# Short-convolution output product by Strassen's algorithm, with block sums by accumulating DMAs

## The chip, the core and the metric

The program runs on one core of one Trainium2 chip. A core has engines that work side by side, each on its own list of instructions in a fixed order: TensorE (PE, matrix products into the accumulators called PSUM), VectorE (DVE, elementwise work on two tensors), ScalarE (ACT, elementwise functions of one tensor), GpSimd (POOL), and SyncE (SP, which here only issues transfers). Transfers between memory and the on-chip store SBUF, or within SBUF, are done by 16 DMA engines; SP's queue and POOL's queue both issue to them. An instruction that needs another engine's result waits for a semaphore, and everything behind it on its own engine waits too.

The metric is device microseconds of one execution, as the median of several runs. Lower is better.

## What is computed

The reference is a two-layer decoder trunk in float32 on 512 tokens of 1024 features. Layer 0 has an attention block and a gated MLP, layer 1 a gated short convolution and a gated MLP; each is added to the residual stream `h`. The change touches only the last line of this function, the product with `w_out` (1024 x 1024):

```python
def short_conv_mixer(h, norm_g, w_in, conv_w, w_out):
    xn = rms_norm(h, norm_g)
    proj = xn @ w_in
    gate_b = proj[..., :CONV_WIDTH]
    gate_c = proj[..., CONV_WIDTH:2 * CONV_WIDTH]
    u = proj[..., 2 * CONV_WIDTH:]
    y = gate_b * causal_dwconv(gate_c * u, conv_w)
    return y @ w_out
```

and `h = h + short_conv_mixer(...)` around it.

## The kernel before

Activations stay in SBUF with features on the 128 partitions and the 512 tokens along the free axis, so 1024 features are eight tiles of [128, 512]. A float32 product is made of three single-pass products of halves: a number is its rounding to a shorter format (`hi`) plus the exact remainder (`lo`), and `mm3` (lines 235 to 240) adds `w_hi x_hi`, `w_hi x_lo` and `w_lo x_hi` into one PSUM accumulator. So each pair of a 128 x 128 weight block and a 512-column activation tile costs three matrix products on PE, each with its own load of stationary weights.

Weights come in float32 in chunks of 512 KB. All chunks are listed in order of use (`want`, lines 207 and 345 to 380). `weights` (line 229) hands out the next one, and keeps two more in preparation: `load` (line 210) issues the transfer on SP's queue (L220), ACT rounds the chunk to `whi` (L223), DVE takes the remainder `wlo` (L226). Each of raw chunk, `whi` and `wlo` has three buffers, used in turn; a buffer that is still read makes the next writer wait.

The short convolution is lines 812 to 843. Its first loop runs over the eight feature tiles; each tile needs three chunks of the input projection (parts u, c and b), every one of them 24 products into one PSUM bank. Then `mix` (lines 816 to 828) multiplies by the row of RMS scales, does the gating and the three-tap convolution on DVE and ACT, and splits the result into `y_hi` and `y_lo` (L320 on ACT, L321 on DVE). The second loop, lines 837 to 842, is the output product: for each of eight output tiles one chunk of `w_out` and 8 x 3 products of 512 columns into one bank (`psa` and `psb` in turn). `residual_out` (line 764) adds the bank to `h` (L765) and feeds the next block's norm (`Norm.feed`, lines 256 to 265): ACT scales and rounds the tile to `hs_hi` (L258), DVE takes the remainder `hs_lo` (L259), ACT squares it (L264) and DVE adds the squares up (L265). `norm.finish` then has the squares summed over features by small products (L292) and the scales spread over the partitions (L278) while the next stage, the up-projection of the second MLP (`up`, line 774), is already running on `hs_hi` and `hs_lo`.

There are eight PSUM banks: two of tag `a`, four of `b`, two of `c`.

What sets the order of the work: `spend` counts an assumed time of the emitted products, and `after` places small work behind a given amount of it. The list of each engine is then fixed when the program is built. A planner goes through the written instructions, and with its own assumed costs puts on each engine the earliest written one that it holds to be ready. So the order on ACT and DVE isn't always the written one: in the profile the scaling of part u of the last feature tile (L819) runs at 798.45 us, ahead of the remainder of a chunk (L226, 799.36 us) whose loading is written before it. On the chip the planned order is kept, whatever the real durations are.

The functions that the diff touches, and what calls them:

Of the kernel before, what the change touches and what calls it, by code (L numbers as in the profile page):

```python
# [49 lines left out]
def trunk(  # L50
# [48 lines left out]
    # a row a column of `gains`: the norms after the first and the conv taps  # L99
# [105 lines left out]
    wanted, ready, at = [], [], [0]  # L205

    def want(dram, k0, nk, c0, n, *more):
        wanted.append((dram, k0, nk, (c0, n) + more))
# [26 lines left out]
    def mm3(acc, w, rhs, first, last):  # L235
        """acc += w.T @ rhs of two pairs of halves."""
# [10 lines left out]
    class Norm:  # L247
        """Gathers the squares of a block's input and gives its RMS scale by token:
        `col` [token, block] on partitions and `row` along the free axis on all of them."""
# [33 lines left out]
        def scaled(self, fn):  # L283
            """Runs what needs `row` when it is there."""
# [14 lines left out]
    def rsqrt(dst, v, n, name):  # L299
        """dst = v ** -0.5 by Newton's method."""  # L300
# [22 lines left out]
    def causal_conv(dst, src, tap):  # L323
        """dst[t] = tap(2) src[t] + tap(1) src[t-1] + tap(0) src[t-2]."""
# [52 lines left out]
    for o in range(ND):  # L377
        want(conv_w_out[0], 0, 8, o * P, P)
# [14 lines left out]
    # ================= attention =================  # L393
# [4 lines left out]
    def choose():  # L398
        """Columns of 0 and 1 that pick the rows of `dl` and `dr`."""
# [25 lines left out]
    def log_gate():  # L425
        """The gates' log-sigmoid, its running sums on the partitions of `dl`."""
# [70 lines left out]
    def queries_keys(p):  # L497
        """Halves of the normed, gained keys and queries of heads 2p and 2p+1. A
        stick-breaking query keeps its scale apart, by token."""
# [63 lines left out]
    def logits(p, b):  # L563
        """Scores and decay of heads 2p and 2p+1 for 128 queries, and what follows up to the weights."""
# [44 lines left out]
    def turn(p, b, ws):  # L609
        """The weights, keys on partitions, in halves."""  # L610
# [19 lines left out]
    def weigh(p, half):  # L630
        """Weights by both halves of the values at once: a head's product has the one
        half on 64 partitions and the other on the rest, which are then added."""
# [98 lines left out]
    # decay: F_q - F_k of a forgetting head as a product of four rows by four. Head  # L731
# [173 lines left out]
```

## Time and profile before

| | |
|---|---|
| time, median of 3 runs (lowest, highest) | 1234.54 us (1233.63, 1237.62) |
| span of the profiled execution, first to last instruction | 1231.8 us |
| time of the profiled execution outside the span | not recorded apart; the median is 2.7 us above the span |
| busy PE / DVE / ACT / POOL | 1214.5 / 762.9 / 500.7 / 21.5 us |
| granted PE clock, mean | 0.997 |
| DMA moved | 108.13 MB, 88 GB/s on average |

Three ways of reading are needed. The profile's page lists groups of instructions by source line, engine and tiles, as out<-in, with the busy time and the mean duration. The timeline lists single instructions by start time in microseconds from the start of the span. A view of windows gives, for a stretch of time, how long each engine was busy. Durations of PE rows are pipelined: two products that follow each other overlap in the rows, and the distance of their starts tells what one costs. On DVE and ACT, too, an instruction can start a little before its predecessor's row ends.

### The profile page before, as it was taken

To read this page: it belongs to the slowest core of one execution; us is meant where nothing else is said; L and a number is where in the kernel's file an instruction comes from. 1 tells how busy PE (TensorE), PEld (TensorE's weight loads), DVE (VectorE), ACT (ScalarE), POOL (GpSimd) and SP (SyncE) were. 2 spreads that over 40 slices of the span, in tenths; PEclk is the share of its full clock that TensorE was granted. 3 is DMA by queue.
4 is the path that set the end of the run, shared out by engine and by line. 5 is a ranking of instruction groups with operands and counts; after the bars stand their busy time and mean duration, and the time that the engine had idled before them with its cause. 6 is when DMAs were issued, how large, how long until landed. Compare 5 with 4: busy or idle time off the path is not lost.

```text
span 1231.8 us, 14998 instructions
## 1 busy us (share of the span) xinstructions
PE 1214.5 (99%) x5861; PEld 987.9 (80%) x5861; DVE 762.9 (62%) x1256; ACT 500.7 (41%) x779; POOL 21.5 (2%) x104
## 2 busy tenths in 40 slices
PE   8999999999999999999999999999999999999998
PEld 7887878767888888888888888888888888888886
DVE  5786878887776777673333555555767776762222
ACT  6455665655443434342222222233444434342120
POOL 3000000000000000000000000000000000000000
PEclk9999999999999999999999999999999999999999
DMA  6312121212333332323333333332333333322330
GB/s 177 104 36 69 36 69 36 69 52 69 95 93 100 89 102 86 103 79 95 94 94 101 91 97 99 89 101 87 91 98 92 96 95 93 98 91 86 118 105 35
DMA packets 183463, 108.13 MB, mean 88 GB/s; under 512 B 4604, under 2 KB 176684, under 8 KB 183392
## 3 DMA queue, kind: packets, MB, share of 16 engines
q1 hardware_dynamic: 183136, 107.01, 29.5%
q8 instruction: 46, 0.75, 0.3%
q0 software_dynamic: 256, 0.16, 0.1%
q14 instruction: 25, 0.20, 0.0%
HBM read 105.06 MB, written 2.10 MB: 87 GB/s over the span
## 4 chain that ended last, share of the span: by engine, by line
PE 94%; DVE 4%; ACT 1%; DMA 1%; issue 0%; SPq 0%; DVEq 0%; ACTq 0%
PE psa L237 13%; PE psa L239 13%; PE psa L238 13%; PE psb L237 11%; PE psb L239 11%; PE psb L238 11%; PE psa L480 3%; PE psa L482 3%; PE psa L481 3%; PE psb L481 2%; PE psb L480 2%; PE psb L482 2%; PE psb L576 1%; DVE rest L603 1%; PE psc L623 1%; PE psa L642 1%
## 5 line engine op out<-in xcount | busy, mean ns | idle before, releaser
L223 ACT ACTIVATE whi<-raw 128x1024 fp32r<-128x1024 f32 (+1 forms) x198 | 208.3, 1053 | 365.9 <-PE psb L238 127.0
L226 DVE TENSOR_TENSOR wlo<-raw,whi 128x1024 fp32r<-128x1024 f32 (+1 forms) x198 | 240.1, 1213 | 162.3 <-ACT whi L223 161.4
L237 PE MATMUL psa<-hs_hi,whi 128*128 128x512 f32 x544 | 220.4, 405 | 0.5 <-DVE o L653 0.5
L239 PE MATMUL psa<-hs_hi,wlo 128*128 128x512 f32 x544 | 215.5, 396 | 0.0
L238 PE MATMUL psa<-hs_lo,whi 128*128 128x512 f32 x544 | 215.0, 395 | 0.0
L237 PE MATMUL psb<-hs_hi,whi 128*128 128x512 f32 x480 | 189.9, 396 | 0.0
L239 PE MATMUL psb<-hs_hi,wlo 128*128 128x512 f32 x480 | 189.8, 395 | 0.0
L238 PE MATMUL psb<-hs_lo,whi 128*128 128x512 f32 x480 | 188.8, 393 | 0.0
L328 DVE SCALAR_TENSOR_TENSOR u<-y,taps,u 128x510 f32<-128x510 f32 (+1 forms) x176 | 131.0, 747 | 3.0
L239 PEld LDWEIGHTS psa<-hs_hi,wlo 128*128 128x128 f32 x544 | 102.2, 188 | 24.0
L237 PEld LDWEIGHTS psa<-hs_hi,whi 128*128 128x128 f32 x544 | 102.7, 189 | 21.8 <-PE psb L582 0.6
L238 PEld LDWEIGHTS psa<-hs_lo,whi 128*128 128x128 f32 x544 | 102.6, 189 | 21.4
L238 PEld LDWEIGHTS psb<-hs_lo,whi 128*128 128x128 f32 x480 | 90.1, 188 | 21.4
L239 PEld LDWEIGHTS psb<-hs_hi,wlo 128*128 128x128 f32 x480 | 90.1, 188 | 21.4
L237 PEld LDWEIGHTS psb<-hs_hi,whi 128*128 128x128 f32 x480 | 90.3, 188 | 20.3
L779 DVE TENSOR_TENSOR y<-psb,nrow_n 128x512 f32<-128x512 f32 x44 | 30.4, 691 | 83.9 <-PE psb L239 83.9
L320 ACT ACTIVATE a<-u 128x512 fp32r<-128x512 f32 x44 | 27.8, 633 | 118.7 <-DVE u L784 118.7
L783 ACT ACTIVATE u<-u 128x512 f32<-128x512 f32 x44 | 27.8, 632 | 91.4 <-DVE u L328 91.4
L325 ACT ACTIVATE u<-y,taps 128x512 f32<-128x512 f32 x88 | 62.9, 717 | 0.0
L321 DVE TENSOR_TENSOR a<-u,a 128x512 fp32r<-128x512 f32 x44 | 30.4, 692 | 29.4 <-ACT a L320 29.4
L480 PE MATMUL psa<-whi,hs_hi 128*128 128x256 f32 (+1 forms) x128 | 38.6, 303 | 0.0
L482 PE MATMUL psa<-whi,hs_lo 128*128 128x256 f32 (+1 forms) x128 | 36.2, 283 | 0.0
(226 smaller groups left out, 1851.0 us busy)
## 6 DMA issues: line engine op xcount, KB each, us to landing
raw<-in_ffn_w_up SPq DMA_DIRECT2D x88, 512.0 KB, 3.8
raw<-in_ffn_w_down SPq DMA_DIRECT2D x30, 512.0 KB, 3.7
raw<-in_attn_w_in SPq DMA_DIRECT2D x24, 512.0 KB, 3.9
raw<-in_conv_w_in SPq DMA_DIRECT2D x24, 512.0 KB, 3.8
raw<-in_ffn_w_down SPq DMA_DIRECT2D x16, 448.0 KB, 3.7
raw<-in_attn_w_out SPq DMA_DIRECT2D x8, 512.0 KB, 3.4
raw<-in_conv_w_out SPq DMA_DIRECT2D x8, 512.0 KB, 3.9
x_tok<-in_x SPq DMA_DIRECT2D x4, 512.0 KB, 7.9
```

The lines of the kernel that those rows point to most:

```text
L223: made = act.activation(hi[:, 0:nk * n], raw[:, 0:nk * n], AF.Copy)
L226: dve.tensor_tensor(lo[:, 0:nk * n], raw[:, 0:nk * n], f32(hi[:, 0:nk * n]), op=ALU.subtract)
L237: pe.matmul(acc, w[0], rhs[0], start=first, stop=False)
L238: pe.matmul(acc, w[0], rhs[1], start=False, stop=False)
L239: pe.matmul(acc, w[1], rhs[0], start=False, stop=last)
L321: dve.tensor_tensor(lo, src, f32(hi), op=ALU.subtract)
L325: act.activation(dst, src, AF.Copy, scale=tap(2))
L328: dve.scalar_tensor_tensor(dst[:, d:], src[:, 0:S - d], tap(j), dst[:, d:], op0=ALU.mult, op1=ALU.add)
L480: pe.matmul(acc, lhs[0], w[0], start=first, stop=False)
L481: pe.matmul(acc, lhs[0], w[1], start=False, stop=False)
L482: pe.matmul(acc, lhs[1], w[0], start=False, stop=last)
L779: dve.tensor_tensor(y, acc, norm.row, op=ALU.mult)
```

## The change

The output product is no longer 8 x 8 x 3 products of 512 columns. It is done in four units, each for two output tiles. In a unit the weights are seen as 2 x 2 blocks (even and odd feature tiles by left and right output tile; a block is four 128 x 128 tiles deep), and the activations as 2 x 2 blocks too (even and odd feature tiles by left and right 256 tokens). Strassen's algorithm, in the form that reuses partial sums, makes the four result blocks from seven block products instead of eight. A block product is 4 x 3 products of 256 columns.

- Activation side (`token_forms`): for each of the four pairs of feature tiles, four sums of blocks are made on DVE (`minus`), and seven forms of 256 columns are split into halves: rounding on ACT, remainder on DVE. They replace `y_hi` and `y_lo` and serve all four units.
- Weight side (`Unit`): four transfers of 256 KB on SP's queue bring the four blocks, into five buffers used in turn. The four sums s1 to s4 are made by two means: ACT copies a block negated (`negative`), and a transfer on POOL's queue adds one SBUF tile onto another (`add`, an accumulating DMA). Seven blocks of a unit are then split into halves, 512 columns at a time, with six buffers each for `hi` and `lo`.
- Result side (`unit_products`): seven block products go into halves of four PSUM banks. ACT copies one, and DVE adds the parts onto the two tiles of `h`. The norm is fed with both tiles after the unit.
- Order: unit 0 is loaded after the fourth feature tile of the first loop, and its sums and halves are written behind the sixth and seventh. The next unit's loads are written at the start of a unit; its sums and halves stand at three points (`steps`) between the block products and after the last. In unit 0 the first three quarters of four block products are emitted ahead of everything that needs the last pair of feature tiles (`early` = 3).
- The eight chunks of `w_out` leave the list of chunks, so `weights` prepares the chunks of the second MLP two ahead from the last input products on.

The rest of the diff takes out comments.

```diff
@@ want
-    for o in range(ND):
-        want(conv_w_out[0], 0, 8, o * P, P)
@@ new
+    HALF = S // 2
+    LEFT, RIGHT = slice(0, HALF), slice(HALF, S)
+    TOKEN_SIDE = {"b11": 0, "b21": 1, "b22": 2, "t1": 3, "t2": 4, "t3": 5, "t4": 6}
+    class Unit:
+        def __init__(self, pool_, dram, k0, n, c0, name):
+            self.pool, self.n, self.name, self.raw, self.halves = pool_, n, name, {}, {}
+            rows = dram[k0 * P:(k0 + 2 * n) * P, c0:c0 + 2 * P].rearrange("(k two p) c -> two p k c", two=2, p=P)
+            for key, half, c in (("s1", 0, 1), ("a11", 0, 0), ("a22", 1, 1), ("a12", 1, 0)):
+                t = pool_.tile([P, 4, P], F32, tag="raw", name=f"raw{key}_{name}", bufs=5)
+                self.raw[key] = t[:, 0:n, :]
+                nc.sync.dma_start(self.raw[key], rows[half, :, :, c * P:(c + 1) * P])
+        def negative(self, key, other, tag, bufs):
+            t = work.tile([P, S], F32, tag=tag, name=f"raw{key}_{self.name}", bufs=bufs)
+            self.raw[key] = t.rearrange("p (k c) -> p k c", c=P)[:, 0:self.n, :]
+            act.activation(self.raw[key], self.raw[other], AF.Copy, scale=-1.0)
+        def add(self, key, other):
+            nc.gpsimd.dma_start(self.raw[key], self.raw[other], accum_op=ALU.add)
+        def sums1(self):
+            self.negative("s3", "s1", "u1", 3)
+            self.negative("s2", "a11", "u1", 3)
+            self.add("s1", "a22")
+            self.add("s3", "a11")
+        def sums2(self):
+            self.add("s2", "s1")
+        def sums3(self):
+            self.negative("s4", "s2", "u0", 2)
+            self.add("s4", "a12")
+        def split(self, *keys):
+            for key in keys:
+                hi, lo = self.halves[key] = [
+                    self.pool.tile([P, 4, P], F32R, tag=n, name=f"{n}{key}_{self.name}", bufs=6)[:, 0:self.n, :]
+                    for n in ("hi", "lo")]
+                act.activation(hi, self.raw[key], AF.Copy)
+                dve.tensor_tensor(lo, self.raw[key], f32(hi), op=ALU.subtract)
+    def token_forms(pool_, hi, lo, even, odd):
+        t = pool_.tile([P, 4, HALF], F32, tag="sums", name="sums", bufs=1)
...
+        first, second = halves_(0, 1, even[:, LEFT]), halves_(1, 3, odd)
+        minus(0, even[:, RIGHT], even[:, LEFT])
+        minus(2, odd[:, RIGHT], even[:, RIGHT])
+        first()
+        second()
+        minus(1, odd[:, RIGHT], t[:, 0, :])
+        minus(3, odd[:, LEFT], t[:, 1, :])
+        halves_(3, 5, flat(t, 0, 2))()
+        halves_(5, 7, flat(t, 2, 4))()
+    def product(acc, unit, a, b, forms, ks=None):
+        w, i = unit.halves[a], TOKEN_SIDE[b]
+        for k in ks or range(unit.n):
+            hi, lo = (x[:, i, :] for x in forms[k])
+            pe.matmul(acc, w[0][:, k, :], hi, start=k == 0, stop=False)
+            pe.matmul(acc, w[0][:, k, :], lo, start=False, stop=False)
+            pe.matmul(acc, w[1][:, k, :], hi, start=False, stop=k == unit.n - 1)
+            spend(0.36)
+    def unit_products(unit, forms, o, name, steps, early=0):
+        x, z = bank("a"), bank("a")
+        w, y = bank("b"), bank("b")
...
+        four = ((z[:, LEFT], "a11", "b11"), (x[:, LEFT], "a12", "b21"), (w[:, LEFT], "s3", "t3"), (y[:, RIGHT], "s1", "t1"))
+        for acc, a, b in four if early else ():
+            product(acc, unit, a, b, forms, range(early))
...
+        rest(0)
+        act.activation(p1u2[:, LEFT], z[:, LEFT], AF.Copy)
+        rest(1)
+        steps[0]()
+        rest(2)
+        product(z[:, RIGHT], unit, "s2", "t2", forms)
+        plus(p1u2[:, RIGHT], z[:, RIGHT], p1u2[:, LEFT])
+        onto(o, slice(0, S), p1u2)
+        plus(u3, w[:, LEFT], p1u2[:, RIGHT])
+        steps[1]()
+        rest(3)
+        both = h[:, o + 1, :].rearrange("p (i c) -> p i c", i=2)
+        plus(both, u3[:, None, :].to_broadcast([P, 2, HALF]), both)
+        product(x[:, RIGHT], unit, "s4", "b22", forms)
+        onto(o, slice(0, S), x)
+        steps[2]()
+        product(y[:, LEFT], unit, "a22", "t4", forms)
+        onto(o, RIGHT, y[:, RIGHT])
+        onto(o + 1, slice(0, S), y)
@@ mix
-            split(y_hi[:, o, :], y_lo[:, o, :], t)
+            mixed_[o] = t
+            if o % 2:
+                token_forms(mp, *forms[o // 2], mixed_[o - 1], t)
@@ first loop
+            if o == 3:
+                unit(0)
+            if o == 5:
+                units[0].sums1()
+            if o == 6:
+                units[0].sums2()
+                units[0].split("a11", "a12", "s3")
+        units[0].split("s1", "s2")
+        units[0].sums3()
         norm = Norm("n3", 8)
-        for o in range(ND):
-            w = weights()
-            acc = bank("ab"[o % 2])
-            for k in range(ND):
-                mm3(acc, (w[0][:, k, :], w[1][:, k, :]), (y_hi[:, k, :], y_lo[:, k, :]), k == 0, k == ND - 1)
-            residual_out(o, acc, norm)
+        for u in range(4):
+            nxt = u + 1 if u < 3 else None
+            if nxt:
+                unit(nxt)
+            def step0():
+                units[u].split("s4")
+                if nxt:
+                    units[nxt].sums1()
+                units[u].split("a22")
+            def step1():
+                if nxt:
+                    units[nxt].sums2()
+                    units[nxt].split("a11", "s3")
+            def step2():
+                if nxt:
+                    units[nxt].sums3()
+            unit_products(units[u], forms, 2 * u, f"co{u}", (step0, step1, step2), 0 if u else 3)
+            if nxt:
+                units[nxt].split("a12", "s2", "s1")
+            for o in (2 * u, 2 * u + 1):
+                norm.feed(o, h[:, o, :])
         norm.finish()
```

`onto(tile, cols, src)` adds `src` to a tile of `h`, `plus` is a DVE addition, `halves_` a rounding on ACT that returns the function which takes the remainder on DVE, and `rest(i)` emits what `early` left of the i-th of the `four` block products.

More of the change, by code (lines that the diff above doesn't have):

```diff
@@ new lines, in product, with plus, onto, rest @@
+    def product(acc, unit, a, b, forms, ks=None):
[9 more added lines that the diff above has]
+        w, y = bank("b"), bank("b")
+        p1u2 = work.tile([P, S], F32, tag="sq", name=f"p1u2_{name}")
+        u3 = work.tile([P, S], F32, tag="nrow", name=f"u3_{name}", bufs=1)[:, LEFT]
+        def plus(dst, src, other):
+            dve.tensor_tensor(dst, src, other, op=ALU.add)
+        def onto(tile_, cols, src):
+            plus(h[:, tile_, cols], src, h[:, tile_, cols])
+        four = ((z[:, LEFT], "a11", "b11"), (x[:, LEFT], "a12", "b21"), (w[:, LEFT], "s3", "t3"), (y[:, RIGHT], "s1", "t1"))
+        for acc, a, b in four if early else ():
+            product(acc, unit, a, b, forms, range(early))
+        def rest(i):
+            acc, a, b = four[i]
+            product(acc, unit, a, b, forms, range(early, unit.n))
+        rest(0)
[17 more added lines that the diff above has]
+        onto(o + 1, slice(0, S), y)
@@ L813, in trunk, with unit @@
     with tc.tile_pool(name="mix", bufs=1) as mp:
-        y_hi = mp.tile([P, ND, S], F32R, tag="y_hi", name="y_hi")
-        y_lo = mp.tile([P, ND, S], F32R, tag="y_lo", name="y_lo")
+        forms = [[mp.tile([P, 7, HALF], F32R, tag=f"y{n}{k}", name=f"y{n}{k}") for n in ("hi", "lo")] for k in range(4)]
+        units, mixed_ = {}, {}
+        def unit(u):
+            units[u] = Unit(mp, conv_w_out[0], 0, 4, 2 * u * P, f"co{u}")
         def mix(o, accs, norm):
```

7 lines of the change are left out of this document (added).

## Prediction

> **What bounds the kernel now.** I read the page first, then the stretch that the change replaces (the output product of the short convolution), then single instructions of each engine in it.
>
> ```profile
> span 1231.8 us, 14998 instructions
> PE 1214.5 (99%) x5861; PEld 987.9 (80%) x5861; DVE 762.9 (62%) x1256; ACT 500.7 (41%) x779; POOL 21.5 (2%) x104
> DVE 5786878887776777673333555555767776762222
> PE 94%; DVE 4%; ACT 1%; DMA 1%; issue 0%; SPq 0%; DVEq 0%; ACTq 0%
> ```
>
> TensorE (PE) sets the time: 94% of the chain that ended last. The third row, VectorE (DVE) by fortieths of the span, never shows more than 8 tenths; that will matter. The span is 1231.8 us, the median of the runs 1234.54: I take 2.7 us lying around the span as unchanged, and add the change of the span to the median.
>
> The first product of `y_hi` and the first product of the next stage (`hs_hi`) enclose the stage:
>
> ```profile
> 809.41 0.40 PE L237 MATMUL psa<-y_hi,whi 128*128 128x512 f32 x1
> ...
> 853.91 0.39 PE L239 MATMUL psb<-y_hi,wlo 128*128 128x512 f32 x1
> 854.14 0.39 PE L237 MATMUL psa<-hs_hi,whi 128*128 128x512 f32 x1
> ```
> ```profile
> core 0: us, PE busy (x) PEld busy (x) DVE busy (x) ACT busy (x) POOL busy (x), PEclk, DMA share, GB/s
> 809.41:854.14 44.73, 44.73 (x193) 36.09 (x192) 24.79 (x31) 17.11 (x24) 0.00 (x0) 1.00 0.33 96
> ```
>
> 192 products of 512 columns (8 tiles x 8 blocks x 3) take 44.73 us, 0.233 us from start to start, at the full granted clock, without a gap. DVE is busy 24.79 of it, ScalarE (ACT) 17.11. The "0.39" of a row is its pipelined duration; only the distance between starts is a price.
>
> **The change: TensorE.** Four units of seven block products replace this; a block product is 4 blocks x 3 products of 256 columns, so 4 x 7 x 12 = 336. The 256-column price is shown in the attention stage, 17 distances between these two:
>
> ```profile
> 83.28 0.28 PE L480 MATMUL psa<-whi,hs_hi 128*128 128x256 f32 x1
> ...
> 85.29 0.28 PE L482 MATMUL psa<-whi,hs_lo 128*128 128x256 f32 x1
> ```
>
> (85.29 - 83.28) / 17 = 0.118 us. 336 x 0.118 = 39.7 us: **5.0 us saved**, all there is to win. A unit lasts 84 x 0.118 = 9.93 us, a block product 1.42.
>
> **VectorE.** Back to back, DVE operations start closer than their durations; the prices are the distances here:
>
> ```profile
> 866.70 0.69 DVE L779 TENSOR_TENSOR y<-psa,nrow_n 128x512 f32<-128x512 f32 x1 [2.19 <-ACT nrow_n L279]
> 867.31 0.68 DVE L779 TENSOR_TENSOR y<-psb,nrow_n 128x512 f32<-128x512 f32 x1
> 867.91 1.22 DVE L226 TENSOR_TENSOR wlo<-raw,whi 128x1024 fp32r<-128x1024 f32 x1
> 869.04 2.73 DVE L328 SCALAR_TENSOR_TENSOR u<-y,taps,u 128x511 f32<-128x511 f32 x4
> ...
> 828.43 0.74 DVE L259 SCALAR_TENSOR_TENSOR hs_lo<-h,gains,hs_hi 128x512 fp32r<-128x512 f32 x1
> 829.10 0.68 DVE L265 TENSOR_TENSOR nacc_n<-nacc_n,sq_n 128x512 f32<-128x512 f32 x1
> ```
> ```profile
> L653 DVE TENSOR_TENSOR o<-psa,o x32: 392/422/428, 76.3 to 283.9; 64x256 f32<-64x256 f32 x32
> ```
>
> 512 columns cost 0.61, 1024 cost 1.13, the scaled remainder L259 0.67; 256 columns last 0.42, and with the 0.08 that the others gain back to back, 0.34. Before, each pair of output tiles had two residual adds, two 1024-column remainders and the norm's feed: 2 x 0.61 + 2 x 1.13 + 2 x (0.67 + 0.61) = 6.0 us in 11.2. In a unit after it are seven remainders (7 x 0.61 = 4.27), four adds of 512 (2.44), three of 256 (1.02) and the feed (2.56): **10.3 us against TensorE's 9.93**. In the last unit there is no next one to prepare, five remainders go: 7.2. So in three units DVE is the longer engine by 0.36, 1.1 us together. Lower bound 0 (remainders may run ahead in slack; unit 0 has five made before the stage), upper bound under the rivals.
>
> [...]
>
> **ScalarE.**
>
> ```profile
> 873.10 0.62 ACT L320 ACTIVATE a<-u 128x512 fp32r<-128x512 f32 x1
> 873.63 0.71 ACT L325 ACTIVATE u<-y,taps 128x512 f32<-128x512 f32 x1
> ...
> 827.16 0.71 ACT L258 ACTIVATE hs_hi<-h,gains 128x512 fp32r<-128x512 f32 x1
> 827.78 0.61 ACT L264 ACTIVATE sq_n<-h 128x512 f32<-128x512 f32 x1
> ```
>
> Seven roundings and three negations at 0.53, a copy of 256 (some 0.3), the feed 2 x (0.62 + 0.53): 7.9 of 9.93 us. Not the bound, but in order: a rounding that waits for a DMA (s4) holds the negations of the next unit and the rounding of a22. Behind it on DVE a remainder without its rounding holds the adds that free the banks of `x` and `z`, which the next unit's second and first products want; on POOL the sum into s1, waiting for its loads, holds those into s3 and s2.
>
> **The last pair's token sums.** They follow the last gate, which stays:
>
> ```profile
> 809.61 0.69 DVE L826 TENSOR_TENSOR cb<-psb,nrow_n 128x512 f32<-128x512 f32 x1 [1.57 <-PE psb L239]
> 810.34 0.69 DVE L827 TENSOR_TENSOR ct<-ct,cb 128x512 f32<-128x512 f32 x1
> ```
>
> The odd tile is there at 811.03. In written order DVE then makes two differences, two remainders and two more differences (4 x 0.34 + 0.34 + 0.61, with some 0.2 of dependence: 813.5); ACT rounds the last (0.63, 814.2) and DVE takes the remainder (0.69): 815.0 with the hand-overs. TensorE has 36 early products (4.26 us, to 813.7) and 6 more before the first that needs it (814.4). Stall 0.6 in written order, 0 if the even tile's part runs earlier: **0.5**. The forms of pairs 0 to 2 and unit 0's loads, sums and halves lie under the input projection, costed at nothing; there DVE is busy 80.75 of 158.00 us, ACT 42.67:
>
> ```profile
> 651.00:809.00 158.00, 158.00 (x688) 127.94 (x687) 80.75 (x109) 42.67 (x48) 0.00 (x0) 1.00 0.33 96
> ```
>
> Without that cover each pair's forms would cost up to the 4 us just counted (811.03 to 815.0).
>
> **The weight sums.** Nothing in this trace accumulates by DMA. The nearest rows:
>
> ```profile
> raw<-in_conv_w_out SPq DMA_DIRECT2D x8, 512.0 KB, 3.9
> out<-r SPq DMA_DIRECT2D x8, 256.0 KB, 2.0
> spare<-in_ffn_conv POOLq DMA_DIRECT2D x4, 33.0 KB, 3.2
> f_bias<-in_attn_f_bias POOLq DMA_DIRECT2D x1, 4.0 KB, 6.3
> spare<-in_ffn_norm POOLq DMA_DIRECT2D x1, 8.0 KB, 1.8
> L107 POOL DMA_DIRECT2D f_bias<-in_attn_f_bias x1 | 0.7, 726 | 0.0
> ```
>
> Call A the time from issue to landing of one sum of 256 KB. It cannot reasonably beat the plain 256 KB store, 2.0; the longest landing of POOL's queue is 6.3. I take **3.3**, by the row it is nearest to in queue and length (3.2). POOL's 0.7 per issue is inside; four a unit are 2.9 of 9.93 us. Per unit three sums hang on each other: s1 += a22, s2 += s1, s4 += a12, and the next but one unit's A11 can only be loaded into s1's buffer when the second has landed. From a unit's start: loads 4.5 (3.9 for 512 KB and a third block behind), two sums 2A, a negation 0.6, a sum A, rounding and remainder 1.4. s4 is needed in the sixth product of the next unit, at 9.93 + 5 x 1.42 = 17.0. Later units add a round each: two blocks loaded (3.5), 2A, 0.5 of hand-overs. The last unit's s4 is then there at 4.5 + 2A + 2 x (4.0 + 2A) + 2.0 + A = 14.5 + 7A, and needed at 17.0 + 2 x 9.93 = 36.9. **Loss 7A - 22.4 above A = 3.2**: 0.7 us at 3.3, 0 at 2.0, 21.7 at 6.3. These late sums and the DVE surplus fall in the same units, and while TensorE waits DVE catches up; I count the larger, 1.1.
>
> [...]
>
> **What moves at no cost.** Eight chunks of the output weights leave the list, so the first two chunks of the next MLP load and split under the last input products, and its third at the MLP's start: 3.8 us of landing, 1.06 and 1.22 of splitting, for a product 11.2 us later (two of 5.6). SP's queue in the stage then holds only unit loads, so their waits delay nobody else. At the end two tiles instead of one are fed at once:
>
> ```profile
> raw<-in_ffn_w_up SPq DMA_DIRECT2D x88, 512.0 KB, 3.8
> ...
> 854.34 0.69 DVE L765 TENSOR_TENSOR h<-psb,h 128x512 f32<-128x512 f32 x1 [2.23 <-PE psb L239]
> ```
>
> Adds of 0.34 and 0.61, rounding 0.62, remainder and feed 0.67 + 0.61 + 0.67 put the last half some 3.7 us behind the last product; the next stage wants it after 21 products, 4.9 us. Late by 1.2 more, it would cost.
>
> **Sum.** -5.0 + 0.5 + 1.1 = -3.4: 1228.4 us of span, **1231.1 us**.
>
> **Rivals.**
> - *Clean*: the remainders run ahead, A is under 3.2. Only 0 to 0.5 is lost: 1229.5 to 1230.0. For it: DVE has 7.2 us in the last unit. Against: 0.36 a unit too much by the rows.
> - *Slow sums* (the other side): the round of load, s1, s2 paces the units. From A = 3.84 on the loss eats the 4.5 us left; at A = 4.5 it is 9.1 and the time 1239.1, at 5.0 12.6 and 1242.6. For it: 6.3 on POOL's queue, and an in-order ACT behind a late s4. Against: 1.8 and 3.2 on the same queue with 2.0 for the bytes.
> - *VectorE-bound with gaps*: its operations depend on ACT, TensorE and DMA in turn; no fortieth of the span shows it above 8 tenths. At 90% a unit takes 10.3 / 0.9 = 11.4: three times 1.5 lost and 0.5, 1234.5, no change.
> - *Nothing gained by 256 columns* (the change would not do what it says): it would need 0.133 us a product; the rows show 0.118. Under 2%, not counted.
>
> **How the numbers follow.** Forecast 0.40, clean 0.22, slow sums 0.25, gaps 0.13. About 0.3% (3.7 us) is what a measurement can tell from no change. The forecast lies just inside it: two fifths of its chance (0.16) and clean make faster 0.38. Same: the rest of the forecast 0.24, gaps 0.13, and 0.03 of slow sums that end near zero: 0.40. Slower 0.22. The range runs from clean less the 0.9 us by which the fastest run was under the median (1228.6) to slow sums at A = 5.0 (1243). The forecast's own range is 1229.5 to 1233.
>
> **What would show it.** 336 products 0.118 apart with 39.7 us of them, no wait on the last pair's forms over 1 us; DVE busy above 9 tenths of the stage; sums landing by 3.3, and TensorE's waits on the halves of s4, below 1 us each. Wrong it is if the landing is past 3.8, if DVE leaves gaps while TensorE waits for it, or if the next stage waits for `hs_lo`.

## The result, and the profile after

The changed kernel takes **1243.68 us** (median, 1243.2 to 1244.5) against 1234.44 of the kernel before on the same chip: a ratio of 1.0069, 95% interval 1.0055 to 1.0083. It is slower by some 9 us where a gain of 3.4 was forecast. The time is 0.7 us above the upper end of the predicted range.

First the head of the page of the changed kernel, then the stretch from the first product of a unit to the first product of the next stage, and the same stretch cut where something changes (columns as before: us, then busy us of each engine, the granted clock, the DMA share, GB/s):

```profile
span 1241.4 us, 15492 instructions
...
PE 1214.6 (98%) x6005; PEld 995.0 (80%) x6005; DVE 788.7 (64%) x1320; ACT 519.8 (42%) x823; POOL 35.5 (3%) x120
...
PEclk9999999999999999999999999989999999999999
```
```profile
811.20:863.58 52.38, 44.41 (x337) 42.84 (x336) 40.12 (x69) 29.48 (x53) 11.26 (x13) 0.93 0.60 122
...
824.00:831.00 7.00, 3.37 (x24) 2.99 (x24) 4.17 (x8) 3.75 (x7) 1.72 (x2) 1.00 0.57 111
831.00:837.80 6.80, 4.62 (x21) 4.63 (x22) 4.96 (x9) 4.31 (x9) 1.00 (x2) 0.50 0.66 156
```

The stage lasts 52.38 us where it lasted 44.73: 7.65 of the 9.6 by which the profiled span grew. From the stage's end to the end of the program nothing changed (1241.4 - 863.58 = 377.8; before 1231.8 - 854.14 = 377.7). Of the 1.8 us ahead of the stage, 0.95 is there at an earlier norm (312.77, now 313.72), long before anything that was changed runs; executions of the kernel before differ by up to 4 us. The other 0.84 comes between the norm ahead of the input projection (682.34, now 683.29) and the stage, and is taken up below. VectorE (DVE) is busy 40.12 of 52.38, so it is not what fills the stage. Between 824 and 831 TensorE (PE) stands half the time, and from 831.0 to 837.8 the granted clock is 0.50.

Where TensorE stands, by its own timeline (start, us, engine, line, operation, idle time before and what ended it):

```profile
822.89 0.28 PE L325 MATMUL psa<-yhi,loa_co 128*128 128x256 f32 x1
824.98 0.36 PE L323 MATMUL psa<-yhi,hia_co 128*128 128x256 f32 x1 [1.81 <-DVE h L337]
...
827.02 0.39 PE L325 MATMUL psa<-yhi,loa_co 128*128 128x256 f32 x1 [0.61 <-DVE loa_co L293]
...
833.17 0.58 PE L323 MATMUL psa<-yhi,his_co 128*128 128x256 f32 x1 [4.21 <-ACT p1u_co L351]
```

These three stalls (6.6 us) lie where unit 0 hands over to unit 1. The 21 products from 833.17 to 837.80 then run at half clock, 0.213 us apart: 4.6 us where 21 x 0.12 = 2.5 would do, 2.1 more. Of the stage's 52.38 us, 336 x 0.12 = 40.3 are products at full clock and 12.1 are lost: 6.6, 2.1, and 3.4 elsewhere, of which 1.2 are three stalls at the last hand-over (0.53, 0.31 and 0.40) and the rest single products that start further apart. The longest stall waits for the copy of `z` (L351) on ScalarE (ACT). Its timeline there:

```profile
829.96 0.63 ACT L292 ACTIVATE his_co<-raws_co 128x512 fp32r<-128x512 f32 x1 [2.18 <-DMA raws_co<-rawa_co]
830.50 0.71 ACT L386 ACTIVATE hs_hi<-h,gains 128x512 fp32r<-128x512 f32 x1
831.11 0.61 ACT L389 ACTIVATE nacc_n<-h 128x512 f32<-128x512 f32 x1
831.63 0.70 ACT L386 ACTIVATE hs_hi<-h,gains 128x512 fp32r<-128x512 f32 x1
832.24 0.61 ACT L392 ACTIVATE sq_n<-h 128x512 f32<-128x512 f32 x1
832.76 0.36 ACT L351 ACTIVATE p1u_co<-psa 128x256 f32<-128x256 f32 x1
```

The rounding of s4 (829.96) waits 2.18 us for its sum to land; behind it in ScalarE's order stand four operations of the norm's feed, and only then the copy that TensorE wants.

How long the sums took from issue to landing, first by the page (medians), then by the DMA view over the burst at 813.0 to 815.6, where three are issued together, and over the quiet end, 847.5 to 860:

```profile
raws_co<-rawa_co POOLq DMA_DIRECT2D x12, 256.0 KB, 4.1
raws_co<-raws_co POOLq DMA_DIRECT2D x4, 256.0 KB, 3.9
...
raws_co<-rawa_co POOLq DMA_DIRECT2D x3, 256.0 KB, 6.4
...
raws_co<-rawa_co POOLq DMA_DIRECT2D x2, 256.0 KB, 3.3
```

Last, the rounds from the sum into s1 of one unit to that of the next, on GpSimd (POOL), VectorE and the load queue (SP), and the load queue's longest wait for a sum (total, times, longest):

```profile
813.09 2.65 POOL L272 DMA_DIRECT2D raws_co<-rawa_co  x3 [27.13 <-DVE ct L957]
820.78 0.86 POOL L272 DMA_DIRECT2D raws_co<-raws_co  x1 [5.04 <-DMA raws_co<-rawa_co]
825.99 0.86 POOL L272 DMA_DIRECT2D raws_co<-rawa_co  x1 [4.36 <-DVE h L337]
...
833.58 0.86 POOL L272 DMA_DIRECT2D raws_co<-rawa_co  x1 [5.17 <-DVE hs_lo L387]
837.66 0.86 POOL L272 DMA_DIRECT2D raws_co<-raws_co  x1 [3.22 <-issue]
...
847.65 0.86 POOL L272 DMA_DIRECT2D raws_co<-rawa_co  x1 [4.21 <-DVE los_co L293]
```
```profile
842.84 1.29 DVE L293 TENSOR_TENSOR los_co<-raws_co,his_co 128x512 fp32r<-128x512 f32 x2 [0.56 <-ACT his_co L292]
```
```profile
844.16 2.25 SPq L264 DMA_DIRECT2D rawa_co<-in_conv_w_out  x2
```
```profile
SPq L264 <- DMA raws_co<-rawa_co: 14.1, 4, 7.6
```

The second round first. The sum into s1 of unit 2 goes out at 833.58 and lands 3.6 later; the sum into s2 goes out at 837.66 and lands 4.0 later, at 841.6. Then ScalarE rounds s2 and s1, VectorE takes their remainders (842.84 to 844.13), and only that frees s1's buffer: the next unit's load goes out at 844.16, lands 2.9 later, and its sum goes out at 847.65. **This round is 14.1 us**, where a unit needs a quarter of a stage, 10 to 11.

The round before it was longer, **19.8 us**. The second sum of the burst, into s1 of unit 1, goes out at 813.76 and takes 6.4; the sum into s2 (820.78) takes 4.3; after a negation the sum into s4 goes out at 825.99 and lands at 829.88. The load that unit 2's sum into s1 needs waits 7.6 us for just that landing, since it goes into the buffer of unit 1's a12, which the sum into s4 reads. It goes out at 829.93 and lands 3.1 later, and the sum follows at 833.58. From 847.65 the last unit's three sums take 11.4 us more: the last one lands at 859.00, 47.8 us after the stage's first product. From 813.76 to there each step waits for the one before it, with a microsecond or less between them apart from the release of s1's buffer.

### The profile page after: what moved, and what is told of

Its sections match the earlier page's. It is cut to its first block, busy times and chain, and to the rows that moved or that the text cites. A ratio compares the mean times of both kernels' runs of the same rounds, so it can differ in the third digit from the quotient of the medians.

```text
span 1241.4 us, 15492 instructions
## 1 busy us (share of the span) xinstructions
PE 1214.6 (98%) x6005; PEld 995.0 (80%) x6005; DVE 788.7 (64%) x1320; ACT 519.8 (42%) x823; POOL 35.5 (3%) x120
## 5 line engine op out<-in xcount | busy, mean ns | idle before, releaser
L226 ACT ACTIVATE whi<-raw 128x1024 fp32r<-128x1024 f32 (+2 forms) x190 | 199.8, 1052 | 321.4 <-PE psb L241 107.4
L229 DVE TENSOR_TENSOR wlo<-raw,whi 128x1024 fp32r<-128x1024 f32 (+2 forms) x190 | 230.3, 1213 | 158.8 <-ACT whi L226 157.8
```

What stands on the lines that cost most here:

```text
L226: made = act.activation(hi[:, 0:nk * n], raw[:, 0:nk * n], AF.Copy)
L229: dve.tensor_tensor(lo[:, 0:nk * n], raw[:, 0:nk * n], f32(hi[:, 0:nk * n]), op=ALU.subtract)
```

## The experiments

Three theories stood against each other at first: the sums land late, and in-order queues carry that to TensorE; the order on ScalarE alone; VectorE is the bound. The times are medians against the kernel before on the same chip, "stage" is the stretch as above. "Sums" are the weight-block sums.

**No sums.** `add` does nothing.

```diff
-            nc.gpsimd.dma_start(self.raw[key], self.raw[other], accum_op=ALU.add)
+            pass
```

> The sixteen accumulating DMAs are left out, and with them the sums of weight blocks: each product is taken with the copied or negated block alone. All products, negations, roundings and feeds stay. Three theories. Late sums (the weight sums land late when several are under way, and the in-order queues of ScalarE and VectorE carry that to TensorE): the gaps of TensorE at 822.9, 826.1 and 828.7 (7.5 us together) shrink below 2 us together, the granted clock stays full in the stage (2.3 us more), and the kernel takes 1233 to 1236 us. Order (the copy of z stands behind the rounding of s4 and four feeds on ScalarE, whatever the sums do): the gap of 4.5 us keeps at least 2 us, 1237 to 1240 us. VectorE is the bound: nothing changes on it, 1242.5 to 1244.5 us.

1232.96 us, ratio 0.9985 (0.9976 to 0.9994). The stage of this run:

```profile
812.02:853.50 41.48, 41.22 (x338) 40.52 (x336) 39.58 (x69) 29.36 (x53) 0.00 (x0) 1.00 0.23 66
```

41.48 us, 3.25 less than before the change: without the sums the stage gains what was forecast, at full clock. VectorE is then busy 39.58 of 41.48 and TensorE still loses little. VectorE as the cause of the loss falls; the sums, with all that waits for them, cost 52.38 - 41.48 = 10.9 us of stage. The time is at the lower end of what was expected of late sums (1233 to 1236). The whole execution gains only 1.8 us by the medians (1234.73 before, on that chip): in the profiled one the stage starts 2.6 us later than before, 0.8 of it again behind that norm and 1.8 ahead of it.

**Small sums, and copies in place of sums.** Which part of a sum's length is it?

```diff
+            nc.gpsimd.dma_start(self.raw[key][:, 0, 0:32], self.raw[other][:, 0, 0:32], accum_op=ALU.add)
```

> Each accumulating DMA adds 32 of 512 columns (16 KB in place of 256 KB); the other columns keep the unsummed block, so a part of each weight sum is left out. Number, order and waits of the DMAs stay. If it is the bytes that make the sums late: landing in about 2 us each, and the time of the run without sums within 1 us. If it is the fixed time of a DMA and the chain of three of them: landings of 2 to 3 us, and at least half of the loss stays, 1238 to 1242 us. VectorE is the bound: 1242.5 to 1244.5 us.

```diff
+            nc.gpsimd.dma_start(self.raw[key], self.raw[other])
```

> The sixteen DMAs of GpSimd copy in place of adding, with the same bytes, order and waits; the additions of weight blocks are left out. If the adding itself makes the DMAs slow: landings of 2 to 3 us with packets of 2 KB at about 84 ns in place of 184, also in the bunch, and 1236.5 to 1239.7 us (as with 16 KB sums or below). If a DMA's fixed time and the bytes make them late: landings within 0.5 us of the adding ones (4.1 median, 6 to 7.6 in the bunch), 1242.5 to 1244.5 us.

Small sums: 1239.71 us, ratio 1.0044 (1.0026 to 1.0061), stage 49.0. Copies: 1237.94, ratio 1.0010 (1.0001 to 1.0020), stage 46.5. The pages' medians, and after the dots the DMA view of the quiet end (from 836 on), first of the small sums, then of the copies:

```profile
raws_co<-rawa_co POOLq DMA_DIRECT2D x12, 16.0 KB, 2.7
raws_co<-raws_co POOLq DMA_DIRECT2D x4, 16.0 KB, 3.5
...
raws_co<-rawa_co POOLq DMA_DIRECT2D x4, 16.0 KB, 2.1
```
```profile
raws_co<-rawa_co POOLq DMA_DIRECT2D x12, 256.0 KB, 2.4
raws_co<-raws_co POOLq DMA_DIRECT2D x4, 256.0 KB, 3.0
...
raws_co<-rawa_co POOLq DMA_DIRECT2D x4, 256.0 KB, 2.3
```

Adding does make the DMA longer (3.3 against 2.3 in the quiet end), but a sixteenth of the bytes still leaves 2.1, and with these lengths 7.5 and 5.0 us of stage are still lost, as was expected if the chain of sums and the adding both count. The second round, from unit 2's sum into s1 to unit 3's, is still 13.4 us in both (829.11 to 842.48, and 830.97 to 844.38). So shortening the DMA as far as was tried here doesn't make this schedule fast enough.

**Rounding of s4 behind the copy of z**, on ScalarE:

```diff
-                act.activation(hi, self.raw[key], AF.Copy)
+                made = act.activation(hi, self.raw[key], AF.Copy)
+                if key == "s4":
+                    behind(made, copies[-1])
...
-        act.activation(p1u2[:, LEFT], z[:, LEFT], AF.Copy)
+        copies.append(act.activation(p1u2[:, LEFT], z[:, LEFT], AF.Copy))
```

> One thing is changed: on ScalarE the rounding of s4 is ordered behind the copy of z's left half (in the changed kernel it stood ahead of it in units 1 and 2); the whole computation stays. Order: the gap of 4.5 us at 828.7 loses the 2.2 us that ScalarE waited for s4 and the rounding's 0.6, the half clock shrinks with it, 1238.5 to 1241 us. Late sums: s4's product waits instead, the gap is moved and not removed, 1242.5 to 1244.5 us. VectorE is the bound: 1242.5 to 1244.5 us.

1243.88 us, ratio 1.0077 (1.0059 to 1.0095): no gain, as the theory of late sums had it. The stall of 4.21 is 1.41 now, and another has come one unit on:

```profile
829.52 0.38 PE L323 MATMUL psa<-yhi,his_co 128*128 128x256 f32 x1 [1.41 <-ACT p1u_co L351]
842.50 0.38 PE L323 MATMUL psb<-yhi,his_co 128*128 128x256 f32 x1 [2.65 <-ACT his_co L292]
```

**An own buffer for s4 of unit 0**, so that its sum is over early and two sums, not three, go out together at the stage's start:

```diff
-            self.negative("s4", "s2", "u0", 2)
+            self.negative("s4", "s2", "sq" if self.name == "co0" else "u0", 2)
```

> Only the buffer of unit 0's negated copy for s4 is another: one that norm n3 uses later, in place of one that the mixing of the last tile holds until 812. The whole computation stays. Bunching theory: s4 of unit 0 is summed before 805, so that two sums in place of three are issued at 813; they land in 3.5 to 5 us in place of 6.4 and 7.6, the chain to s4 of unit 1 is 2 to 3 us earlier, the three gaps of 7.5 us fall to 3 to 5, 1238 to 1241 us. The chain alone (an accumulating DMA is slow whatever else is under way, three in a row are too long): landings of 4 us or more stay and the gaps lose under 1.5 us, 1242 to 1244 us. VectorE is the bound: 1242.5 to 1244.5 us.

1245.12 us, ratio 1.0072 (1.0057 to 1.0087), above what either theory gave. The first hand-over is nearly clean (0.35 and 0.82 idle), and the loss sits at the second:

```profile
840.96 0.39 PE L323 MATMUL psb<-yhi,his_co 128*128 128x256 f32 x1 [2.40 <-ACT his_co L292]
...
845.57 0.58 PE L323 MATMUL psa<-yhi,his_co 128*128 128x256 f32 x1 [3.16 <-ACT p1u_co L351]
```

So the bunching alone was not the cause either. Twice a stall taken away at one hand-over came back at the next: something paces the units, and this pointed to the rounds. The last sum of this run lands 46.6 us after the stage's first product, hardly sooner than the 47.8 of the changed kernel.

**GpSimd sums**, without and with the own buffer:

```diff
-            self.negative("s3", "s1", "u1", 3)
-            self.add("s3", "a11")
+            combine(self, "s3", "a11", "s1", "u1", 3)
...
+    def combine(self, key, x, y, tag, bufs):
+        t = work.tile([P, S], F32, tag=tag, name=f"raw{key}_{self.name}", bufs=bufs)
+        self.raw[key] = t.rearrange("p (k c) -> p k c", c=P)[:, 0:self.n, :]
+        pool.tensor_tensor(self.raw[key], self.raw[x], self.raw[y], op=ALU.subtract)
```

s2 and s4 are made in the same way, and s1 by an addition in place.

> The four sums of a unit are taken by GpSimd (one 512-column operation each, subtraction included) in place of ScalarE's negation and the accumulating DMA; the whole computation stays. Late sums: with an operation of 0.6 to 2 us in place of 3.3 to 7.6 us to land, the three gaps shrink below 3 us together, 1234 to 1238 us. Order: a gap of at least 2 us stays ahead of z's right half, 1237 to 1240 us. VectorE is the bound: no gain, 1243 us or more, and more still where GpSimd's reads slow VectorE's operations.

> The sums are taken by GpSimd as in the earlier run (1.3 to 1.9 us each there), and s4 of unit 0 has the other buffer, so that no sum of unit 0 is left for the moment of the last pair's forms (there the first gaps of 1.06 and 2.04 us began, and the granted clock fell). The whole computation stays. Late sums: those two gaps go and with them the half clock: 1236 to 1239 us. If GpSimd's own sums slow VectorE (77 operations took 54.9 us in the window from 811 to 870, 75 took 43.8 with the DMAs): gaps stay above 3 us together, 1239 to 1241 us.

1241.11 (ratio 1.0053, 1.0034 to 1.0072), between the ranges expected, and 1239.30 (1.0035, 1.0024 to 1.0046), as expected if GpSimd slows VectorE. A sum takes GpSimd 1.3 to 2.3 us, where a sum by DMA takes 3.3 alone, but VectorE pays: its groups in the first of these runs, 811 to 860 (in its slowest execution, 1243.63), and its stage in the second:

```profile
L387 DVE SCALAR_TENSOR_TENSOR hs_lo<-h,gains,hs_hi 128x512 fp32r<-128x512 f32 x6 | 6.4, 1062 | 0.0
L393 DVE TENSOR_TENSOR nacc_n<-nacc_n,sq_n 128x512 f32<-128x512 f32 x5 | 5.6, 1110 | 0.0
...
L337 DVE TENSOR_TENSOR h<-psa,h 128x512 f32<-128x512 f32 x3 | 2.0, 679 | 0.0
```
```profile
811.78:860.76 48.98, 43.11 (x338) 40.93 (x336) 47.97 (x68) 24.20 (x42) 15.19 (x10) 1.00 0.19 56
```

VectorE is busy 47.97 of 48.98 us: here it is the bound, made so by the sums on GpSimd.

**Seven buffers** for weight blocks, in the same memory (the token sums, which had 4 KB of a partition to themselves, take two of them in turn), unit 1 loaded before the last pair's forms, and the own buffer of s4; then the same with the rounding of s4 behind the copy of z:

```diff
-                t = pool_.tile([P, 4, P], F32, tag="raw", name=f"raw{key}_{name}", bufs=5)
+                t = pool_.tile([P, 4, P], F32, tag="raw", name=f"raw{key}_{name}", bufs=7)
...
-        t = pool_.tile([P, 4, HALF], F32, tag="sums", name="sums", bufs=1)
+        t = [pool_.tile([P, 4, P], F32, tag="raw", name=f"sums{n}", bufs=7).rearrange("p k c -> p (k c)") for n in range(2)]
...
             if o == 6:
                 units[0].sums2()
                 units[0].split("a11", "a12", "s3")
+                unit(1)
...
-            if nxt:
+            if nxt and u:
                 unit(nxt)
```

> Seven buffers for the weight blocks in place of five (the token sums of a pair take two of the same buffers in turn, where they had one of their own), unit 1 loaded ahead of the last pair's forms, and the own buffer of s4 in unit 0. Same operations; the whole computation stays. Theory of the round (a buffer is loaded again only when s1 of the unit before has been summed, has served s2 and is rounded; load, sum, sum and rounding make a round of 14 us where TensorE needs 11.4): the round is broken, the transitions between units lose 3 us together or less, a stage of 43 to 46 us, 1234.5 to 1238 us. Theory of the long chain alone (three sums one behind the other are too long, wherever the loads start): the sums are no earlier against the products, 1241 to 1244 us. VectorE is the bound: 1242.5 to 1244.5 us.

> As the run with seven buffers, and on ScalarE the rounding of s4 stands behind the copy of z. Theory of the round: s4 is no longer late, so the order matters little, within 1 us of that run. Order: 1 to 3 us below it, since the copy of z no longer waits for s4 and TensorE not for the copy.

1240.96 (1.0053, 1.0038 to 1.0068) and 1241.04 (1.0049, 1.0032 to 1.0066). That is 2.7 us won by the medians and some 2 by the ratios, whose intervals overlap with the changed kernel's; 1234.5 to 1238 was asked for by the theory of the round, and 1241 to 1244 by that of the long chain alone. The sums do come sooner: the last one lands 41.7 and 37.7 us after the stage's first product, where it was 47.8. So how late the last sum lands no longer explains the time by itself. Most of what is lost in the second run lies at one place. ScalarE's timeline there:

```profile
845.54 0.63 ACT L269 ACTIVATE raws_co<-raws_co 128x512 f32<-128x512 f32 x1 [5.60 <-DMA raws_co<-raws_co]
846.08 0.36 ACT L351 ACTIVATE p1u_co<-psa 128x256 f32<-128x256 f32 x1
```

The negation for the next unit's s4 waits 5.60 us for the sum into s2 at the head of ScalarE's queue, with the copy of z behind it; TensorE stands 4.30 us. The planner that orders each engine had put it there.

**Seven buffers and the orders together.** The negation of s4 goes behind the copy of z as well, and a12 is rounded ahead of it, with a11 and s3. In the first of two runs the feeds of the norm also go behind the next unit's roundings of s4 and a22.

```diff
-            act.activation(self.raw[key], self.raw[other], AF.Copy, scale=-1.0)
+            made = act.activation(self.raw[key], self.raw[other], AF.Copy, scale=-1.0)
+            if key == "s4" and copies:
+                behind(made, copies[-1])
...
-                    units[nxt].split("a11", "s3")
+                    units[nxt].split("a11", "s3", "a12")
...
-                units[nxt].split("a12", "s2", "s1")
+                units[nxt].split("s2", "s1")
```

> The seven buffers, unit 1 loaded early, and what waits late on ScalarE set behind what TensorE wants soon: rounding and negation of s4 behind the copy of z, the rounding of a12 ahead of the negation of s4, the feeds of the norm behind the next unit's roundings. The whole computation stays. If buffers and queue orders together make the loss: no gap over 1.5 us, granted clock full, a stage of 42 to 45 us, 1233 to 1236.5 us. If the sums' own length is the cause whatever the order: gaps of 3 us or more remain, 1239 to 1242 us. If VectorE then is the bound: busy over 9.5 tenths of the stage with gaps of under 1 us each, 1236 to 1239 us.

> As the ordered run, but the feeds of the norm stand where they stood, ahead of the copy of z. The whole computation stays. If the feeds on ScalarE and VectorE hold the banks of the next unit: 1 to 3 us above the ordered run. If they lie beside other work: within 0.7 us of it.

With the feeds where they stood: **1232.79 us, ratio 0.9974 (0.9962 to 0.9987)**, faster than the kernel before by 0.26%, with an interval that excludes no change. It is 5.3 us below the run with the feeds moved, where no difference or 1 to 3 us above it was expected. Its stage:

```profile
810.80:853.35 42.55, 41.35 (x337) 40.59 (x336) 39.75 (x69) 27.90 (x51) 8.67 (x10) 1.00 0.68 139
```

42.55 us at full clock, 1.1 above the run without sums. A sum takes no less time to land than in the changed kernel:

```profile
raws_co<-rawa_co POOLq DMA_DIRECT2D x12, 256.0 KB, 4.7
raws_co<-raws_co POOLq DMA_DIRECT2D x4, 256.0 KB, 4.1
```

But the sums start sooner, and the last one lands 36.4 us after the stage's first product.

With the feeds moved it takes 1238.07 (1.0016, 1.0007 to 1.0024), against the expectation. The traced execution of this run is its slowest, 1241.12, so the size of what it shows is not the median's. Between a feed's rounding and its square the planner had now put the negation of s4, waiting 1.47 us for a DMA; VectorE's next addition waits for that square, and the remainder that TensorE wants is behind the addition. ScalarE, VectorE and TensorE in turn:

```profile
845.64 0.63 ACT L269 ACTIVATE raws_co<-raws_co 128x512 f32<-128x512 f32 x1 [1.47 <-DMA raws_co<-raws_co]
```
```profile
846.82 0.69 DVE L393 TENSOR_TENSOR nacc_n<-nacc_n,sq_n 128x512 f32<-128x512 f32 x1 [2.37 <-ACT sq_n L392]
...
848.37 0.68 DVE L293 TENSOR_TENSOR loa_co<-rawa_co,hia_co 128x512 fp32r<-128x512 f32 x1
```
```profile
849.10 0.58 PE L325 MATMUL psa<-yhi,loa_co 128*128 128x256 f32 x1 [3.88 <-DVE loa_co L293]
```

The same move of the feeds on the run with the own buffer alone had gone the other way:

> The own buffer of s4 in unit 0, and the feeds of the next norm (four ScalarE and four VectorE operations a unit) are issued after the next unit's s4 and a22 are rounded, so that they no longer stand ahead of its copy of z on ScalarE. The whole computation stays. If the queue order of ScalarE adds to the late sums: 1 to 3 us below the kernel with the own buffer alone. If the sums alone set the gaps: within 0.7 us of it.

1242.18 us (1.0054, 1.0036 to 1.0071), 2.9 below that run by the medians, as expected if ScalarE's order adds to the late sums, though the intervals of the ratios overlap. An order seems to be good or bad by what else waits in the queue; this pair was not followed through its traces.

**The orders without the buffers** complete the four cases:

> The orders on ScalarE of the best run (rounding and negation of s4 behind the copy of z, rounding of a12 ahead of the negation of s4), but the five buffers, the shared buffer of unit 0's s4 and the loads of unit 1 of the changed kernel. The whole computation stays. If the order alone makes the loss (the buffers gave 2.7 us by themselves): 1234 to 1237 us. If the round through five buffers is a limit of its own, as reckoned from the trace (14 us a round against 11.4): 1239 to 1243 us, with gaps of 2 to 3 us at each transition.

**1249.25 us**, ratio 1.0112 (1.0095 to 1.0129), worse than expected by either theory. ScalarE's wait for the sum into s2 is longer than ever, its stage is the longest, and its last sum lands 50.4 us after the stage's first product:

```profile
842.70 0.63 ACT L269 ACTIVATE raws_co<-raws_co 128x512 f32<-128x512 f32 x1 [6.77 <-DMA raws_co<-raws_co]
```
```profile
811.46:868.64 57.18, 46.65 (x338) 44.63 (x337) 40.13 (x69) 29.30 (x53) 11.27 (x13) 0.91 0.54 112
```

| | planner's order | orders set by hand |
|---|---|---|
| five buffers | 1243.7 (1.0069) | 1249.3 (1.0112) |
| seven buffers, unit 1 early, own s4 | 1241.0 (1.0053) | 1232.8 (0.9974) |

In the two runs with five buffers the last sum lands late (47.8 and 50.4 us into the stage), and putting what waits for the sums in another place only makes something else wait. With seven the sums come sooner (41.7 and 36.4), but gain only 2 to 2.7 us while the planner's order puts a waiting operation ahead of what TensorE needs. The loss is of both together: 10.9 us by the medians, or 0.95% by the ratios, between the changed kernel and the best. Some half a microsecond of it is not in the stage: in the seven-buffer runs TensorE doesn't stall at the norm ahead of the input projection. The seven buffers, the early unit 1 and the own s4 buffer were only run as one. The own s4 buffer alone won nothing (1245.12), but five buffers with it and with the set orders were not run; how the three share it is open.

## Why the prediction was wrong

**Right.** 336 products at 0.12 us: (41.48 - 1.2 us of gaps) / 336 in the run without sums, 0.118 forecast; the saving is 4.4 us and not 5.0. VectorE above 9 tenths, with about its forecast load (39.6 us; forecast 3 x 10.3 + 7.2 = 38.1), once the sums are away. No wait on the last pair's forms in the changed kernel: TensorE has no stall until 822.89. The feeds at the end cost the next stage nothing (377.8 against 377.7 us). Without sums the stage is 3.25 us shorter, and the sum was -3.4. That they agree so well is luck in part: a smaller saving (4.4 for 5.0) and smaller losses (1.2 for 1.6) cancel.

**The step that failed** is the round in the weight sums: "two blocks loaded (3.5), 2A, 0.5 of hand-overs", with the buffer free "when the second has landed". At the forecast A = 3.3 that is 10.6 us; the two rounds lasted 19.8 and 14.1. From unit 1's sum into s1 to the landing of the last sum the forecast has 2 x 10.6 + 0.6 + 3 x 3.3 = 31.7 us, and the trace 859.00 - 813.76 = 45.2: 13.5 more, 9.2 of it in the first round and 3.5 in the second. The chain began 1.9 us sooner than forecast (2.6 us into the stage and not 4.5), and the forecast had the last s4 0.7 late: 13.5 - 1.9 + 0.7 makes it some 12 us late, about what TensorE lost (12.1; 10.9 more than without sums).

The first round has three sums in it and not two (6.4, 4.3 and 3.9), since the load waits for a buffer that the sum into s4 reads; the first of them was slowed in the burst. The second round is 14.07 = 3.55 + 0.53 + 3.97 + 2.53 + 2.93 + 0.56 (sum, hand-over, sum, release, load, hand-over). The release was left out: s1's buffer is free only after its own rounding, behind a negation and another rounding on ScalarE, and its remainder on VectorE, 2.53 us. The loads were put too high by 0.6, the hand-overs too low by 0.6. So this round is 2A + 6.55 and not 2A + 4.0. In the runs with copies and with small sums this gives 4.49 + 2.30 + 6.55 = 13.3 and 2.68 + 3.42 + 6.55 = 12.7 by their own landings, where 13.4 was measured in both. In a unit of 10.4 us (41.48 / 4) it leaves A = 1.9, below the 2.1 of a 16 KB sum alone; the forecast had it free up to 3.2. No length that was measured here is free.

**A itself** was guessed well for a sum alone (3.3, measured 3.3; luck in part, as no row of before adds by DMA) and badly for the kernel: 4.1 at the median and 6.4 in the burst, where three sums, and a load beside them, were under way together. The forecast named the point from which it would be wrong, a landing past 3.8. By the formula 4.1 costs 7 x 4.1 - 22.4 = 6.3 us; 10.9 were lost.

**What the forecast priced at nothing.** It said that on ScalarE a rounding waiting for a DMA holds what stands behind it, and gave that no price: the 4.21 us come from the copy of z, which stands behind s4 and four operations of the feeds, and the orders decide over 8.2 us once there are seven buffers (1241.0 to 1232.8). It took the granted clock as full: half clock after the stalls is 2.1 us. And "the forms and unit 0's halves lie under the input projection" is wrong in one place. In the norm's chain of small operations the planner put unit 0's first remainders. VectorE, before:

```profile
682.34 0.15 DVE L269 TENSOR_SCALAR nv_n<-psc 128x4 f32<-128x4 f32 x1
...
684.58 0.16 DVE L316 SCALAR_TENSOR_TENSOR ncol_n<-rb_n,ry_n 128x4 f32<-128x4 f32 x1
```

and after:

```profile
683.29 0.15 DVE L397 TENSOR_SCALAR nv_n<-psc 128x4 f32<-128x4 f32 x1
684.37 0.69 DVE L293 TENSOR_TENSOR loa_co<-rawa_co,hia_co 128x512 fp32r<-128x512 f32 x1 [0.93 <-ACT hia_co L292]
...
687.03 0.16 DVE L444 SCALAR_TENSOR_TENSOR ncol_n<-rb_n,ry_n 128x4 f32<-128x4 f32 x1
```

2.24 us from the first to the last became 3.74, and TensorE stands 0.57 us for it at 687.34, most of the 0.84 that is lost between there and the stage.

**The rivals.** *Slow sums* is what happened, with its mechanism, "the round of load, s1, s2 paces the units"; by its formula a loss of 10.9 us takes A = (10.9 + 22.4) / 7 = 4.8, where the median was 4.1, since its rounds were too short. *VectorE-bound with gaps* falls: VectorE has gaps because it waits too (from 811 to 860 for ScalarE's `his_co` 6.2 us and `hs_hi` 3.4). *Clean* comes nearest in the run with seven buffers and set orders, which gains 2.8 us on its chip (1235.6 to 1232.8) where *clean* asked for 4.5 to 5.0.

That the rounds and the in-order queues make the loss is shown by the traces and by the two changes together; how much of the 10.9 us is the rounds' and how much the queues' cannot be told apart, since each change needs the other.

## What to carry to other kernels

Work that hides needs a round, not a latency: count everything from a buffer's load to its release, the roundings that read it last included, against the time of one step (here 14.1 against 10.4 us), and give it more buffers before a faster engine. An operation that waits for a DMA costs what stands behind it on its engine (here ScalarE's negation waited 5.60 us, and TensorE stood 4.30 for the copy behind it), so look at each queue for what waits at its head; an automatic order can put such an operation ahead of what the bound engine needs, as it did here (why the planner did, no run shows). Test buffers and order together: here the one alone gave 2 to 2.7 us, the other lost 5.6, and both won 10.9.

## What was not expected of the hardware

An accumulating DMA of 256 KB within SBUF took 3.3 us alone, 1.0 more than the same DMA without the adding (2.3), and 6.4 (median of three) when three were under way. The sums went as packets of 2 KB at a median of 184 ns each, the copies as half as many of 4 KB at some 170 ns (an estimate: the queue's 17.1% of 16 engines from 836 to 860 are 65.7 us, for 384 of these packets and 96 small ones), so the two differ in their packets too. The 16 KB sums took 2.1 in the quiet end (median of four): a sixteenth of the bytes saves 1.2 of the 3.3.

VectorE's operations with both operands in SBUF took 1062 and 1110 ns while GpSimd added (L387 and L393 above), against 747 and 685 in the changed kernel; the one that reads PSUM kept 679 (684 in the changed kernel). Of VectorE's rows from 811 to 860 only such with both operands in SBUF grew, the longest from 1219 to 2303 ns (the remainder of a 1024-column chunk, L229); why, no run shows.

Stalls of 1.81, 0.61 and 4.21 us within 11 us went with 6.8 us of half clock (0.50 from 831.0 to 837.8); in the run with small sums a stall of 2.91 us did not (1.00 over the whole stage). What makes the clock fall was not tried.
